# Scores of two heads in the two halves of TensorE's rows, and the first layer's memory products one group of self heads later

## Chip, cores, metric

One core of one Trainium2 chip. The metric is the device time of one execution in microseconds (us). In every stretch quoted below the granted TensorE clock is 1.00, its 2.4 GHz level.

## What is computed

A trunk of two layers on 256 tokens of width 1024, in fp32. Each layer mixes tokens with 12 self heads of width 64 and 4 heads that look into 256 memory tokens, adds the output projection to the residual stream, and then runs a SwiGLU layer of width 2816. The first layer's self attention adds a running sum of log gates, the second a distance penalty. Cut to one layer's mixing:

```python
proj = rms_norm(h, norm_mix[i]) @ w_in          # queries, keys, values of 12 heads, memory queries (and gates)
mkv = rms_norm(mem, norm_mem[i]) @ w_mem_kv[i]  # keys and values of 4 memory heads
s = q @ k.T * 64 ** -0.5 + F[t] - F[s]          # first layer; the second: - slope * (t - s); causal
self_out = softmax(s) @ v
mem_out = softmax(qm @ mk.T * 64 ** -0.5) @ mv
h = h + concat(self_out, mem_out) @ w_out[i]
h = h + (silu(hn @ w_gate) * (hn @ w_up)) @ w_down[i]
```

## The kernel before

All products keep fp32 accuracy with fp32r operands: a matrix is split into `hi`, its rounding, and `lo`, the rest, and a product is three matmuls (hi·hi, lo·hi, hi·lo, `prod`). ScalarE (ACT) writes `hi`, VectorE (DVE) the difference `lo`; that is done for activations as well as for the weights, which are streamed from memory in units of up to 1 MB (`Plan`, `fetch`, L207) and split in halves up to five halves ahead of use (`split`, L227 and L230).

TensorE (PE) and SyncE (SP) run in the order in which the code is written (`manual_schedule`, L770); for ACT, DVE and GpSimd (POOL) a scheduler sets the order, save at the start of the first layer. While PE works through the projections, it calls `step()` (L464) after every two k-blocks, which moves each active head pair one step on. `attend` (L394) is such a pair: it lets `idle` steps pass (table `IDLE`, L58), writes the scores of two heads into two PSUM banks (L405 to L409), then DVE and ACT do the softmax (L412 to L431); two or three steps later PE transposes the probabilities (L438), ACT and DVE copy them out of PSUM (L442, L443), and two steps later PE multiplies by the values (L447 to L451). The value products go into halves of the array's columns, 64 for each head (`128*64` in the profile); all other products use the array whole (`128*128`).

A score product contracts over 64 values only. Before the change the other 64 rows are filled so that one matmul does two of the three terms: rows of the head's own half hold `hi` of its queries and the other half holds `lo` (`split_queries`, L378), against keys whose `hi` stands in both halves and whose `lo` stands in one, with zeros beside it (`split_keys`, L386; `no_lo`, L334). A pair so takes eight matmuls of 256 columns, and its operands take six ACT copies and two DVE and two POOL subtractions of 64x256, and two POOL memsets.

In the first layer the order is: values, queries and keys of group 0 of the self heads (two pairs in a group), then `memory_heads` (L547: memory keys and values, L343, and memory queries), then groups 1 and 2 (`MEM_AT`, L55), then the output projection in the order 3, 0, 1, 2 of its row blocks (block 3 is that of the memory heads, L609). The second layer has the same order, with its memory keys and values made earlier, after the first layer's SwiGLU. The gates' running sums go through memory: `gate_sums` (L515) multiplies them out on PE, writes `fr` to `fd` (L522) and reads it back to all partitions as `fk` (L528), which the first layer's softmax needs (`bias`, L530).

Of the kernel before, what the change touches and what calls it, by code (L numbers as in the profile page):

```python
# [22 lines left out]
F32 = mybir.dt.float32  # L23
# [59 lines left out]
class Plan:  # L83


    def __init__(self, a):
# [4 lines left out]
        for i in range(2):  # L91
# [8 lines left out]
            for g in range(3):  # L100
# [5 lines left out]
                U["qk", i, g] = [self.unit([w[:, :SW], w[:, SW:]], 4 * u, 4, g * 2 * P, 2 * P) for u in range(2)]  # L106
            U["out", i] = [self.unit([a["w_out"][i]], 2 * j, 2, 0, D) for j in (3, 0, 1, 2)]
            U["gu", i], U["dn", i] = {}, {}
# [33 lines left out]
def trunk(ctx: ExitStack, tc: tile.TileContext, plan, stream, x, gains, norm_final, square, mem, out):  # L142
# [22 lines left out]

    mem_t = [ap.tile([P, 2, 512], F32, tag="probs", name=f"mem{t}", bufs=3).rearrange("p a s -> p (a s)") for t in range(NT)]

# [77 lines left out]
    def split_ps(hi, lo, ps, scale=None):  # L245

        if scale is None:
            nc.scalar.activation(hi, ps, AF.Copy)
            nc.vector.tensor_sub(lo, ps, hi.bitcast(F32))  # L249
# [79 lines left out]
    fk = cp.tile([P, H, S], F32, name="fk")  # L329
    mks = [cp.tile([P, 2, 2 * S], F32R, name=f"mk{p}") for p in range(HM // 2)]  # L330
# [3 lines left out]
    def no_lo(dst):  # L334

        for a in range(2):
            nc.gpsimd.memset(dst[HOME[1 - a], a, S:].bitcast(F32), 0.0)

# [4 lines left out]
    def mem_kv(i):  # L343
# [31 lines left out]

    ENG = (nc.gpsimd, nc.vector)

    def split_queries(dst, q):  # L378

        for a in range(2):  # L380
            nc.scalar.activation(dst[HOME[a], a], q[HOME[a]], AF.Copy)
        for a in range(2):
            r = ENG[a].tensor_sub(dst[HOME[1 - a], a], q[HOME[a]], dst[HOME[a], a].bitcast(F32))
        return r

    def split_keys(dst, k):  # L386

        for a in range(2):
            nc.scalar.activation(dst[HOME[a], a, :S], k[HOME[a]], AF.Copy)
            nc.scalar.activation(dst[HOME[1 - a], a, :S], k[HOME[a]], AF.Copy)  # L390
        for a in range(2):
            ENG[a].tensor_sub(dst[HOME[a], a, S:], k[HOME[a]], dst[HOME[a], a, :S].bitcast(F32))

    def attend(name, xq, xk, vt, h0, idle, bias, dst, kt):  # L394

# [8 lines left out]
        sb = [bank(f"s_{name}_{a}") for a in range(2)]  # L404
        for a in range(2):  # L405
# [5 lines left out]
        pr = ap.tile([P, 2, 512], F32, tag="probs", name=f"p_{name}", bufs=3)  # L411
        with tc.high_priority(offset=URGENT):  # L412
# [26 lines left out]
        pT = ap.tile([P, 2, 512], F32, tag="probs", name=f"pT_{name}", bufs=3)  # L439
        width = len(blocks) * P  # L440
# [29 lines left out]
    def mixer(i, xs, rs):  # L470
# [44 lines left out]
        def gate_sums():  # L515
            yield
            fb = bank("F_ps")
            fb.mm(fb.t[:H, 0:S], lf[:, 0], prefix)
            fb.mm(fb.t[:H, P:S], lf[:, 1], prefix[:, 0:P], stop=True)
            fr = ap.tile([P, 2, S], F32, tag="work", name="fr", bufs=WORK_BUFS)[:H, 0]  # L520
            nc.vector.tensor_copy(fr, fb.t[:H, :S])
            nc.sync.dma_start(fd, fr)  # L522
            wake_exp(fr[:, 0:1])
            yield
            yield
            for g in range(GATE_PARTS):
                hs = slice(g * (H // GATE_PARTS), (g + 1) * (H // GATE_PARTS))
                nc.sync.dma_start(fk[:, hs], fd[hs].unsqueeze(0).to_broadcast([P, H // GATE_PARTS, S]))  # L528

        def bias(h0):  # L530

            b = fk[:, h0:h0 + 2]
            if i == 1:
                return b[:, :, P:], b

            b0 = ap.tile([P, 2, P], F32, tag="bias", name=f"bias{h0}", bufs=1)
            for t, o in enumerate((b0, b[:, :, P:])):
                with tc.issue_after(mem_done[i]):
                    nc.vector.tensor_add(o, b[:, :, t * P:(t + 1) * P], mask[:, P:].unsqueeze(1).to_broadcast([P, 2, P]))
            return b0, b  # L540
# [6 lines left out]
        def memory_heads():  # L547
# [14 lines left out]
            qm = ap.tile([P, 2, S], F32, tag="work", name=f"qm{i}", bufs=WORK_BUFS)  # L562
            nc.vector.tensor_mul(qm, qb.t.rearrange("p (a s) -> p a s", a=2), rsb[:, 0:1, :].to_broadcast([P, 2, S]))
            for p in range(HM // 2):
                xq = ap.tile([P, 2, S], F32R, tag="work", name=f"xqm{i}{p}", bufs=WORK_BUFS)
                mem_done[i] = split_queries(xq, qm[:, p]).ins
                active.append(attend(f"m{i}{p}", xq, mks[p], mvs, 2 * p, IDLE_MEM[i] + p, None, hT, 6 + p))

        for g in range(3):
# [3 lines left out]
            for k in range(KD):  # L573
# [6 lines left out]
                if k % 2:  # L580
                    step()
            if i == g == 0:
                rs_mem.extend(factor(mem_t[t], f"mem{t}") for t in range(NT))
# [4 lines left out]
            for a in range(2):  # L588
                p = 2 * g + a
                qk = ap.tile([P, 2, S], F32, tag="work", name=f"qk{i}{p}", bufs=WORK_BUFS)  # L590
                nc.vector.tensor_mul(qk.rearrange("p a s -> p (a s)"), kb[a].t, rsb.rearrange("p a s -> p (a s)"))
                xq = ap.tile([P, 2, S], F32R, tag="work", name=f"xq{i}{p}", bufs=WORK_BUFS)
                xk = ap.tile([P, 2, 2 * S], F32R, tag="pair", name=f"xk{i}{p}", bufs=PAIR_BUFS)
                no_lo(xk)
                split_queries(xq, qk[:, 0])
                split_keys(xk, qk[:, 1])
                idle = a + IDLE[i][g]
                active.append(attend(f"s{i}{p}", xq, xk, vsb, 2 * p, idle, bias, hT, p))

# [8 lines left out]

        for n, j in enumerate((3, 0, 1)):  # L609
            for kk in range(2):  # L610
# [34 lines left out]
    def ffn(i, xs, late):  # L645
# [5 lines left out]
        def gu(c, kk):  # L651
# [13 lines left out]
            if first:  # L665
                rsb.append(spread(rs, f"f{i}", (1.0,), "f")[:, 0])
            if kk == 0:
# [102 lines left out]
    with tc.manual_schedule(engines={PE, SP}):  # L770
        warm = ap.tile([P, 512], BF16, tag="work", name="warm", bufs=WORK_BUFS)
        nc.gpsimd.memset(warm, 0.0)
        for mk in mks:
            no_lo(mk)
        wb = bank("warm_ps")
# [47 lines left out]
```

## Time and profile before

| | |
|---|---|
| median of three runs | 621.79 us (621.36 to 622.78) |
| the profiled execution: time, span | 621.42 us, 619.6 us |
| busy share of the span: PE, DVE, ACT, POOL | 98%, 73%, 63%, 10% |
| matmuls | 3634 |

How to read the rows: matmuls are pipelined. One of 256 columns is shown as taking 0.28 us, but in an undisturbed row of them one starts every 0.12 us. A stall of PE therefore shows an idle time that is 0.16 us shorter than the time lost. "Chain" is the chain of waits that ended last: at each step the work that the end was waiting for.

### The profile page before, as it was taken

What the parts mean: (1) busy time and instruction counts of PE and PEld (TensorE: products, weight loads), DVE (VectorE), ACT (ScalarE), POOL (GpSimd) and SP (SyncE); (2) the same over time, 40 slices, a digit from 0 to 9 for tenths busy, and PEclk for the clock granted to TensorE, in tenths of its full rate; (3) what the DMA queues carried; (4) which work ended last, traced back from release to release, by engine and by line L of the source; (5) the groups of instructions that cost most, each with busy time, mean ns of one, the idle gap of its engine ahead of it and who ended that gap; (6) DMA issues with size and microseconds to landing.
All of it is one profiled execution on the core that took longest, in us unless ns stands there. A gap on an engine that the chain in (4) does not pass through costs nothing.

```text
span 619.6 us, 9546 instructions
## 1 busy us (share of the span) xinstructions
PE 606.8 (98%) x3634; PEld 533.0 (86%) x3634; DVE 452.7 (73%) x815; ACT 393.2 (63%) x736; POOL 63.4 (10%) x90
## 2 busy tenths in 40 slices
PE   9999899999999999999999999999999999999995
PEld 6999888788888888888899998877888888888884
DVE  5677999687676776668675589986866766667664
ACT  6889788485555555557467589776755555555542
POOL 2032112055000000000011032110000000000000
PEclk9999999999999999999999999999999999999999
DMA  8977452335544554556355731332445555456301
GB/s 349 422 283 278 165 179 95 135 137 204 199 172 179 197 204 181 177 190 227 126 200 191 272 137 69 136 136 103 170 177 197 205 195 178 177 197 205 136 1 68
DMA packets 16774, 112.31 MB, mean 181 GB/s; under 512 B 1996, under 2 KB 2008, under 8 KB 4312
## 3 DMA queue, kind: packets, MB, share of 16 engines
q1 hardware_dynamic: 16440, 111.42, 49.0%
q8 instruction: 28, 0.46, 0.3%
q10 hardware_dynamic: 288, 0.29, 0.1%
q14 instruction: 18, 0.15, 0.1%
HBM read 110.64 MB, written 1.06 MB: 180 GB/s over the span
## 4 chain that ended last, share of the span: by engine, by line
PE 88%; DVE 5%; ACT 4%; issue 2%; POOL 0%; POOLq 0%; DVEq 0%; ACTq 0%
PE gu L183 40%; PE d_acc L183 18%; PE qk_ps L183 8%; PE o_acc L183 7%; PE v_ps L183 6%; DVE lo L230 2%; PE s_s L183 1%; ACT hi L227 1%; PE pT_s L438 1%; PE o_s L183 1%; PE mv_ps L183 1%; PE qm_ps L183 1%; PE mk_ps L183 1%; PE warm_ps L183 1%; DVE p_m L431 1%
## 5 line engine op out<-in xcount | busy, mean ns | idle before, releaser
L230 DVE TENSOR_TENSOR lo<-raw,hi 128x1024 fp32r<-128x1024 f32 (+3 forms) x201 | 239.7, 1198 | 67.0 <-ACT hi L227 62.1
L227 ACT ACTIVATE hi<-raw 128x1024 fp32r<-128x1024 f32 (+3 forms) x201 | 206.5, 1035 | 71.3 <-PE d_acc L183 46.8
L183 PE MATMUL gu<-x_ffn,hi 128*128 128x512 f32 x704 | 177.4, 392 | 0.0
L183 PEld LDWEIGHTS gu<-x_ffn,hi 128*128 128x128 f32 x704 | 126.3, 189 | 22.2
L183 PE MATMUL d_acc<-hi,h 128*128 128x512 f32 x348 | 107.1, 389 | 0.0
L183 PEld LDWEIGHTS gu<-x_ffn,lo 128*128 128x128 f32 x704 | 96.7, 190 | 8.1 <-ACT x_ffn L251 1.0
L183 PE MATMUL gu<-x_ffn,lo 128*128 128x256 f32 x704 | 100.5, 284 | 0.1
L183 PEld LDWEIGHTS d_acc<-hi,h 128*128 128x128 f32 x348 | 65.3, 188 | 13.6
L183 PE MATMUL qk_ps<-x_x,hi 128*128 128x256 f32 x384 | 72.4, 284 | 2.1 <-ACT p_m L427 2.1
L183 PE MATMUL d_acc<-lo,h 128*128 128x512 f32 x174 | 67.7, 389 | 0.0
L183 PEld LDWEIGHTS qk_ps<-x_x,hi 128*128 128x128 f32 x384 | 61.0, 191 | 3.3 <-ACT p_m L427 2.5
L183 PE MATMUL qk_ps<-x_x,lo 128*128 128x256 f32 x192 | 54.3, 283 | 0.0
L672 ACT ACTIVATE gate<-gu 128x256 f32<-128x256 f32 x44 | 16.9, 384 | 57.6 <-PE gu L183 57.6
L672 ACT ACTIVATE up<-gu 128x256 f32<-128x256 f32 x44 | 16.9, 385 | 39.7 <-PE gu L183 39.5
L183 PE MATMUL o_acc<-hi,x_hT 128*128 128x512 f32 x128 | 41.6, 404 | 0.3 <-DVE x_hT L249 0.3
L183 PEld LDWEIGHTS d_acc<-lo,h 128*128 128x128 f32 x174 | 32.7, 188 | 6.8
L673 DVE TENSOR_TENSOR gate<-gu,gate 128x256 f32<-128x256 f32 x44 | 18.7, 424 | 25.6 <-ACT gate L672 25.5
L183 PEld LDWEIGHTS qk_ps<-x_x,lo 128*128 128x128 f32 x192 | 36.8, 191 | 0.0
L673 DVE TENSOR_TENSOR up<-gu,up 128x256 f32<-128x256 f32 x44 | 18.7, 424 | 24.6 <-ACT up L672 24.6
L183 PE MATMUL v_ps<-hi,x_x 128*128 128x384 f32 (+1 forms) x128 | 33.1, 339 | 0.0
L183 PEld LDWEIGHTS o_acc<-hi,x_hT 128*128 128x128 f32 x128 | 22.9, 188 | 5.9 <-DVE x_hT L249 1.0
L427 ACT ACTIVATE p_s<-p_s,nmax_s 128x128 f32<-128x128 f32 (+1 forms) x48 | 21.3, 445 | 9.8 <-DVE nmax_s L417 9.7
(152 smaller groups left out, 752.2 us busy)
## 6 DMA issues: line engine op xcount, KB each, us to landing
raw<-in_stream SPq DMA_DIRECT2D x94, 1024.0 KB, 4.8
raw<-in_stream SPq DMA_DIRECT2D x3, 1036.0 KB, 7.9
raw<-in_stream SPq DMA_DIRECT2D x4, 768.0 KB, 4.5
fk<-fd SPq DMA_DIRECT2D x3, 512.0 KB, 7.5
raw<-in_stream SPq DMA_DIRECT2D x2, 518.0 KB, 4.4
h<-in_x SPq DMA_DIRECT2D x2, 512.0 KB, 11.9
mem<-in_mem SPq DMA_DIRECT2D x2, 512.0 KB, 12.5
gfin<-in_norm_final SPq DMA_DIRECT2D x1, 512.0 KB, 3.6
```

What stands on the lines that cost most here:

```text
L183: nc.tensor.matmul(o, lhsT, rhs, start=self.fresh, stop=stop, skip_group_check=True)
L227: nc.scalar.activation(hi[:, c0:c1], src[:, c0:c1], AF.Copy)
L230: nc.vector.tensor_sub(lo[:, c0:c1], src[:, c0:c1], hi[:, c0:c1].bitcast(F32))
L427: nc.scalar.activation(pr[:, a, c], src, AF.Exp, bias=nmax[:, a, j], scale=scale, accum_out=total[:, a, j])
L431: nc.vector.tensor_scalar_mul(pr[:, a, c], pr[:, a, c], rc[:, a, qt:qt + 1])
L438: nc.tensor.transpose(tb[a].t[:, n * P:(n + 1) * P], pr[:, a, c:c + P], ident)
L672: nc.scalar.activation(v[:, 1], b[s].t[:, S:], AF.Copy)
L673: nc.vector.tensor_add(v[:, 0], b[s].t[:, :S], v[:, 1])
```

## The change

1. `split_queries`, `split_keys`, `no_lo` and the duplicated operands go. `split_ps` (one ACT copy and one DVE subtraction, L245) splits a pair's queries and keys together in one 128x512 operation each, so head 0 lies in partitions 0 to 63 and head 1 in 64 to 127; the four memory heads' keys are split the same way (`mks`), and their queries too (`xm`). POOL has no part in it any more.
2. `attend` makes twelve score matmuls for a pair instead of eight, each on 64 rows by 128 columns of the array, those of the two heads in turn.
3. The first layer's memory products move behind group 1 (`MEM_AT`); its `IDLE` tables and the order of its output projection are set to suit (`OUT_ORDER`), and `gate_sums` starts one step earlier. In the second layer the tables' values stay what they were.
4. `probs` gets four buffers (was three). A pair's operands (`xp`, `xm`) take one `pair` buffer of three.

```diff
-MEM_AT = (1, 1)
+MEM_AT = (2, 1)
-IDLE = ((7, 2, 2), (3, 2, 2))
-IDLE_MEM = (1, 1)
+IDLE = (((5, 6), (4, 5), (2, 3)),
+        ((3, 4), (2, 3), (2, 3)))
+IDLE_MEM = ((2, 3), (1, 2))
+OUT_ORDER = ((0, 1, 3, 2), (3, 0, 1, 2))
...
-        for p in range(HM // 2):
-            split_keys(mks[p], mk[:, p])
+        split_ps(mks[:, 0], mks[:, 1], mk)
...
-        for a in range(2):
-            for qt in range(NT):
-                o, q = sb[a].t[:, qt * S:(qt + 1) * S], slice(qt * P, (qt + 1) * P)
-                sb[a].mm(o, xq[:, a, q], xk[:, a, :S])
-                sb[a].mm(o, xq[:, a, q], xk[:, a, S:], stop=True)
+        for qt in range(NT):
+            o, q = slice(qt * S, (qt + 1) * S), slice(qt * P, (qt + 1) * P)
+            for n, (st, mv) in enumerate(((xq[0], xk[0]), (xq[1], xk[0]), (xq[0], xk[1]))):
+                for a in range(2):
+                    sb[a].mm(sb[a].t[:, o], st[HOME[a], q], mv[HOME[a]], stop=n == 2)
...
         def gate_sums():
-            yield
             fb = bank("F_ps")
...
-                xq = ap.tile([P, 2, S], F32R, tag="work", name=f"xq{i}{p}", bufs=WORK_BUFS)
-                xk = ap.tile([P, 2, 2 * S], F32R, tag="pair", name=f"xk{i}{p}", bufs=PAIR_BUFS)
-                no_lo(xk)
-                split_queries(xq, qk[:, 0])
-                split_keys(xk, qk[:, 1])
+                xp = ap.tile([P, 2, 2, S], F32R, tag="pair", name=f"xp{i}{p}", bufs=PAIR_BUFS)
+                split_ps(xp[:, 0], xp[:, 1], qk)
```

PE in the first layer, where the first self pair's scores (`s_s`) stand. Before, after the fourth k-block of group 1, beside a memory pair's (`s_m`):

```order
L183 MATMUL qk_ps_753<-x_x_81,hi_0_629 128x256
L183 MATMUL s_s_0_871<-xk_485,xq_484 128x256 x4
L183 MATMUL s_s_1_872<-xk_485,xq_484 128x256 x4
L183 MATMUL s_m_0_899<-mk_87,xqm_747 128x256 x4
L183 MATMUL s_m_1_900<-mk_87,xqm_747 128x256 x4
```

In the changed program, the last two of the twelve, which now stand between memory keys and values (`mk_ps`, `mv_ps`):

```order
L185 MATMUL s_s_0_704<-xp_465 128x256
L185 MATMUL s_s_1_705<-xp_465 128x256
L185 MATMUL mk_ps_633<-x_mem_626,hi_0_513 128x256
L185 MATMUL mk_ps_633<-x_mem_626,lo_0_514 128x256
L185 MATMUL mk_ps_633<-x_mem_626,hi_0_513 128x256 x2
```

The first scores moved from group 1's projection to the middle of the memory keys, and the two heads alternate. Over the whole first layer the scores now stand alone between products on the whole array five times, and beside a value product three times; in the second layer four times alone (once two pairs together), three times beside one value product or between two.

ACT in the first layer, at the split of group 0's first pair. Before:

```order
L227 ACTIVATE hi_0_376<-raw_328 128x1024
L227 ACTIVATE hi_2_404<-raw_328 128x1024
L381 ACTIVATE xq_484<-qk_482 64x256
L389 ACTIVATE xk_485<-qk_482 64x256
L390 ACTIVATE xk_485<-qk_482 64x256
```

and in the changed program:

```order
L229 ACTIVATE hi_0_429<-raw_331 128x1024
L250 ACTIVATE xp_465<-qk_463 128x512
L250 ACTIVATE xp_470<-qk_468 128x512
L229 ACTIVATE hi_2_475<-raw_331 128x1024
L253 ACTIVATE x_mem_626<-raw_321,gT 128x256
```

One row for a pair stands where six copies were.

DVE in the second layer, from the memory queries (`qm`) to the maxima of the first memory pair's scores (`nmax_m`). Before:

```order
L563 TENSOR_TENSOR qm_3823<-qm_ps_3764,rsb_x_3729 128x512
L392 TENSOR_TENSOR xk_3751<-qk_3748,xk_3751 64x256
L230 TENSOR_TENSOR lo_2_3838<-raw_3565,hi_2_3837 128x1024
L383 TENSOR_TENSOR xqm_3825<-qm_3823,xqm_3825 64x256
L383 TENSOR_TENSOR xqm_3830<-qm_3823,xqm_3830 64x256
L230 TENSOR_TENSOR lo_0_3868<-raw_3638,hi_0_3867 128x1024
L230 TENSOR_TENSOR lo_2_3924<-raw_3638,hi_2_3923 128x1024
L420 TENSOR_REDUCE nmax_m_3905<-s_m_0_3895 128x1 x2
L420 TENSOR_REDUCE nmax_m_3905<-s_m_1_3896 128x1 x2
```

and in the changed program:

```order
L541 TENSOR_TENSOR qm_3735<-qm_ps_3676,rsb_x_3663 128x512
L232 TENSOR_TENSOR lo_0_3773<-raw_3572,hi_0_3772 128x1024
L251 TENSOR_TENSOR xm_3737<-qm_3735,xm_3737 128x512
L232 TENSOR_TENSOR lo_2_3833<-raw_3572,hi_2_3832 128x1024
L232 TENSOR_TENSOR lo_0_3927<-raw_3630,hi_0_3926 128x1024
L399 TENSOR_REDUCE nmax_m_3814<-s_m_0_3800 128x1 x2
L399 TENSOR_REDUCE nmax_m_3814<-s_m_1_3801 128x1 x2
```

Three subtractions of 64x256 went and one of 128x512 came; three weight splits stand on the way in both.

SP's queue in the first layer, from the memory loads (`mem`) to the gates' way through memory (`fd`, `fk`). Before (raw_237 and raw_328 are the memory heads' key and value weights, raw_340 to raw_555 those of groups 1 and 2):

```order
L207 DMA raw_237<-in_stream 128x2048
L199 DMA mem_79<-in_mem 128x1024
L199 DMA mem_80<-in_mem 128x1024
L207 DMA raw_328<-in_stream 128x2048
L207 DMA raw_338<-in_stream 128x2048
L207 DMA raw_340<-in_stream 128x2048
L207 DMA raw_374<-in_stream 128x2048
L207 DMA raw_432<-in_stream 128x2048
L207 DMA raw_555<-in_stream 128x2048
L522 DMA fd<-fr 12x256
L207 DMA raw_627<-in_stream 128x2048
L528 DMA fk<-fd 128x1024 x3
```

and in the changed program, where group 1's two units stand ahead of this piece, raw_321 is the memory itself, raw_331 and raw_367 its weights, raw_427 and raw_511 group 2:

```order
L209 DMA raw_321<-in_stream 128x2048
L209 DMA raw_331<-in_stream 128x2048
L201 DMA mem_79<-in_mem 128x1024
L201 DMA mem_80<-in_mem 128x1024
L209 DMA raw_367<-in_stream 128x2048
L209 DMA raw_425<-in_stream 128x2048
L209 DMA raw_427<-in_stream 128x2048
L500 DMA fd<-fr 12x256
L209 DMA raw_511<-in_stream 128x2048
L506 DMA fk<-fd 128x1024 x3
```

The memory's transfers moved behind group 1's, and the gates' write went one unit forward, ahead of group 2's second unit.

## Rows read from the trace of the kernel before

**Rows 1.** Page, part 1: busy us (share of the span) and instructions

```profile
PE 606.8 (98%) x3634; PEld 533.0 (86%) x3634; DVE 452.7 (73%) x815; ACT 393.2 (63%) x736; POOL 63.4 (10%) x90
```

**Rows 2.** Stretches: busy us of PE, PEld, DVE, ACT, POOL; clock; DMA share, GB/s

```profile
48.00:60.00 12.00, 12.00 (x102) 12.00 (x102) 8.54 (x10) 11.60 (x21) 1.95 (x3) 1.00 0.79 290
60.00:66.00 6.00, 5.15 (x43) 4.95 (x42) 5.94 (x10) 3.18 (x5) 1.99 (x2) 1.00 1.01 393
72.00:78.00 6.00, 4.09 (x33) 3.88 (x33) 5.92 (x27) 5.78 (x21) 1.90 (x2) 1.00 0.00 0
78.00:96.00 18.00, 18.00 (x142) 15.46 (x141) 17.88 (x48) 14.89 (x36) 4.22 (x6) 1.00 0.50 177
376.00:382.00 6.00, 4.87 (x42) 4.66 (x41) 5.89 (x19) 5.64 (x16) 1.89 (x2) 1.00 0.48 176
```

**Rows 3.** Timeline of PE at its stalls: start, us, [idle before, what ended it]

```profile
60.03 0.28 PE L183 MATMUL qk_ps<-x_x,hi 128*128 128x256 f32 x1
61.16 1.10 PE L183 MATMUL s_m<-mk,xqm 128*128 128x256 f32 x7 [0.85 <-POOL xqm L383]
...
73.04 0.38 PE L183 MATMUL qk_ps<-x_x,hi 128*128 128x256 f32 x1 [1.18 <-ACT p_m L427]
...
74.89 0.39 PE L183 MATMUL qk_ps<-x_x,hi 128*128 128x256 f32 x1 [0.88 <-ACT p_m L427]
...
379.18 0.63 PE L438 MATMUL pT_m<-sq,p_m 128*128 128x128 f32 x4 [1.14 <-DVE nmax_s L417]
```

**Rows 4.** Chain of waits in order of time: start us, us, what

```profile
23.95 11.51 PE qk_ps L183 x96
...
78.19 2.87 PE qk_ps L183 x24
...
81.71 1.02 PE o_m L183 x8
82.73 3.07 PE qk_ps L183 x24
...
101.27 0.95 PE s_s L183 x8
```

**Rows 5.** Timeline of PE and PEld in narrow windows at one value product

```profile
86.39 0.43 PE L183 MATMUL o_m<-pT_m,mv 128*64 128x256 f32 x1
...
86.39 0.44 PE L183 MATMUL o_m<-pT_m,mv 128*64 128x256 f32 x2
...
86.39 0.66 PE L183 MATMUL o_m<-pT_m,mv 128*64 128x256 f32 x4
...
86.39 0.13 PEld L183 LDWEIGHTS o_m<-pT_m,mv 128*64 128x64 f32 x1 [0.17 <-DVE lo L230]
...
86.39 0.15 PEld L183 LDWEIGHTS o_m<-pT_m,mv 128*64 128x64 f32 x2 [0.17 <-DVE lo L230]
```

**Rows 6.** Groups by line and shape: xcount | busy us, mean ns | idle before

```profile
L227 ACT ACTIVATE hi<-raw 128x1024 fp32r<-128x1024 f32 x184 | 193.0, 1056 | 62.2 <-PE d_acc L183 46.8 <-PE qk_ps L183 6.3 <-PE o_acc L183 6.1
...
L389 ACT ACTIVATE xk<-qk 64x256 fp32r<-64x256 f32 x24 | 10.0, 416 | 0.4
L381 ACT ACTIVATE xq<-qk 64x256 fp32r<-64x256 f32 x24 | 10.0, 415 | 4.1 <-DVE qk L591 3.7
...
L383 DVE TENSOR_TENSOR xq<-qk,xq 64x256 fp32r<-64x256 f32 x12 | 8.1, 678 | 1.5 <-ACT xq L381 1.2
L591 DVE TENSOR_TENSOR qk<-qk_ps,rsb_x 128x512 f32<-128x512 f32 x12 | 8.0, 679 | 1.6 <-ACT rsb_x L283 1.6
...
L392 DVE TENSOR_TENSOR xk<-qk,xk 64x256 fp32r<-64x256 f32 x12 | 5.8, 481 | 1.2 <-ACT xk L389 0.9
```

**Rows 7.** Timeline of SP's queue, and the page's DMA issues (last: us to landing)

```profile
48.20 0.43 SPq L522 DMA_DIRECT2D fd<-fr  x1
...
52.92 1.28 SPq L528 DMA_DIRECT2D fk<-fd  x3
...
fk<-fd SPq DMA_DIRECT2D x3, 512.0 KB, 7.5
```

More of the change, by code (lines that the diff above doesn't have):

```diff
@@ L106, in __init__ @@
                 U["qk", i, g] = [self.unit([w[:, :SW], w[:, SW:]], 4 * u, 4, g * 2 * P, 2 * P) for u in range(2)]
-            U["out", i] = [self.unit([a["w_out"][i]], 2 * j, 2, 0, D) for j in (3, 0, 1, 2)]
+            U["out", i] = [self.unit([a["w_out"][i]], 2 * j, 2, 0, D) for j in OUT_ORDER[i]]
             U["gu", i], U["dn", i] = {}, {}
@@ L163, in trunk @@
     nc.gpsimd.memset(minus_half, -0.5)
-    mem_t = [ap.tile([P, 2, 512], F32, tag="probs", name=f"mem{t}", bufs=3).rearrange("p a s -> p (a s)") for t in range(NT)]
+    mem_t = [ap.tile([P, 2, 512], F32, tag="probs", name=f"mem{t}", bufs=4).rearrange("p a s -> p (a s)") for t in range(NT)]
     def load_x():
@@ L329, in trunk @@
     fk = cp.tile([P, H, S], F32, name="fk")
-    mks = [cp.tile([P, 2, 2 * S], F32R, name=f"mk{p}") for p in range(HM // 2)]
+    mks = cp.tile([P, 2, HM // 2, S], F32R, name="mks")
     mvs = [cp.tile([P, HM, DH], F32, name=f"mv{t}") for t in range(NT)]
     HOME = [slice(a * DH, (a + 1) * DH) for a in range(2)]
-    def no_lo(dst):
-        for a in range(2):
-            nc.gpsimd.memset(dst[HOME[1 - a], a, S:].bitcast(F32), 0.0)
     rs_mem = []
@@ L373, in mem_kv @@
         yield
[L376 to L392, printed above, removed]
     def attend(name, xq, xk, vt, h0, idle, bias, dst, kt):
@@ L404, in attend @@
         sb = [bank(f"s_{name}_{a}") for a in range(2)]
-        for a in range(2):
-            for qt in range(NT):
-                o, q = sb[a].t[:, qt * S:(qt + 1) * S], slice(qt * P, (qt + 1) * P)
-                sb[a].mm(o, xq[:, a, q], xk[:, a, :S])
-                sb[a].mm(o, xq[:, a, q], xk[:, a, S:], stop=True)
+        for qt in range(NT):
[3 more added lines that the diff above has]
+                    sb[a].mm(sb[a].t[:, o], st[HOME[a], q], mv[HOME[a]], stop=n == 2)
         nmax = sp.tile([P, 2, NT], F32, tag="nmax", name=f"nmax_{name}")
-        pr = ap.tile([P, 2, 512], F32, tag="probs", name=f"p_{name}", bufs=3)
+        pr = ap.tile([P, 2, 512], F32, tag="probs", name=f"p_{name}", bufs=4)
         with tc.high_priority(offset=URGENT):
@@ L537, in bias @@
             for t, o in enumerate((b0, b[:, :, P:])):
-                with tc.issue_after(mem_done[i]):
+                with tc.issue_after(mem_done[i]) if i in mem_done else nullcontext():
                     nc.vector.tensor_add(o, b[:, :, t * P:(t + 1) * P], mask[:, P:].unsqueeze(1).to_broadcast([P, 2, P]))
@@ L563, in memory_heads @@
             nc.vector.tensor_mul(qm, qb.t.rearrange("p (a s) -> p a s", a=2), rsb[:, 0:1, :].to_broadcast([P, 2, S]))
+            xm = ap.tile([P, 2, HM // 2, S], F32R, tag="pair", name=f"xm{i}", bufs=PAIR_BUFS)
+            mem_done[i] = split_ps(xm[:, 0], xm[:, 1], qm).ins
             for p in range(HM // 2):
-                xq = ap.tile([P, 2, S], F32R, tag="work", name=f"xqm{i}{p}", bufs=WORK_BUFS)
-                mem_done[i] = split_queries(xq, qm[:, p]).ins
-                active.append(attend(f"m{i}{p}", xq, mks[p], mvs, 2 * p, IDLE_MEM[i] + p, None, hT, 6 + p))
+                active.append(attend(f"m{i}{p}", (xm[:, 0, p], xm[:, 1, p]), (mks[:, 0, p], mks[:, 1, p]), mvs, 2 * p,
+                                     IDLE_MEM[i][p], None, hT, 6 + p))
         for g in range(3):
@@ L581, in mixer @@
                     step()
-            if i == g == 0:
+            if i == 0 and g == MEM_AT[0] - 1:
                 rs_mem.extend(factor(mem_t[t], f"mem{t}") for t in range(NT))
@@ L591, in mixer @@
                 nc.vector.tensor_mul(qk.rearrange("p a s -> p (a s)"), kb[a].t, rsb.rearrange("p a s -> p (a s)"))
-                xq = ap.tile([P, 2, S], F32R, tag="work", name=f"xq{i}{p}", bufs=WORK_BUFS)
-                xk = ap.tile([P, 2, 2 * S], F32R, tag="pair", name=f"xk{i}{p}", bufs=PAIR_BUFS)
-                no_lo(xk)
-                split_queries(xq, qk[:, 0])
-                split_keys(xk, qk[:, 1])
-                idle = a + IDLE[i][g]
-                active.append(attend(f"s{i}{p}", xq, xk, vsb, 2 * p, idle, bias, hT, p))
+                xp = ap.tile([P, 2, 2, S], F32R, tag="pair", name=f"xp{i}{p}", bufs=PAIR_BUFS)
+                split_ps(xp[:, 0], xp[:, 1], qk)
+                idle = IDLE[i][g][a]
+                active.append(attend(f"s{i}{p}", (xp[:, 0, 0], xp[:, 1, 0]), (xp[:, 0, 1], xp[:, 1, 1]), vsb, 2 * p, idle, bias, hT, p))
         acc = [[bank(f"o_acc{i}{t}{c}") for c in range(2)] for t in range(NT)]
@@ L607, in o_item @@
                 prod(acc[t][c], acc[t][c].t, tok(hT, k, t), (wh[:, 0, cs], wl[:, 0, cs]), n == 3 and kk == 1)
-        for n, j in enumerate((3, 0, 1)):
+        for n, j in enumerate(OUT_ORDER[i][:3]):
             for kk in range(2):
@@ L772, in trunk @@
         nc.gpsimd.memset(warm, 0.0)
-        for mk in mks:
-            no_lo(mk)
         wb = bank("warm_ps")
```

6 lines of the change are left out of this document (3 added, 3 removed).

## Prediction

> **What bounds the kernel now.** I read the page's busy shares first, then busy times by stretch, then the timeline of PE alone where a stretch shows it idle, and the chain of waits for prices. PE is busy 98% of the span [rows 1], at the full clock, and undisturbed it starts a matmul of 256 columns every 11.51 / 96 = 0.12 us [rows 4]. So two things alone can move the end: what PE itself has to do, and the few places where it stands still. In both layers these lie in the attention. In the first layer PE loses time between 60 and 78 us, in the second between 376 and 382 us [rows 2]. In each of these stretches DVE is busy nearly without a break (5.94, 5.92 and 5.89 of 6.00 us), while from 48 to 60 us, just before, it has 3.5 us of 12 free [rows 2]. DVE's work is not too much for the layer, it is bunched.
>
> The stalls, one by one [rows 3]. A matmul of 256 columns is shown with 0.28 us and starts every 0.12, so a stall costs its idle time and 0.16 us, and about 0.1 more, since the first matmul behind it shows 0.38 where others show 0.28. First layer: the memory scores wait for POOL's part of the query split, 0.85 idle; group 2's projection waits twice for the exponentials of the second memory pair, whose two score banks it is to reuse, 1.18 and 0.88 idle. That is 0.85 + 1.18 + 0.88 + 3 x 0.26 = **3.7 us**. Second layer: the second memory pair's transposes wait for DVE, 1.14 + 0.26 = **1.4 us**. Together 5.1 us.
>
> **The change part by part.**
>
> *Splits.* For one self pair ACT now makes six copies of 0.416 us, 2.5 us [rows 6]. Then it makes one of 128x512; between the copy of 256 columns (0.416) and the one of 1024 (1.056) [rows 6] that is about 0.63, so 1.9 us less. DVE makes 0.68 + 0.48 = 1.16 us now and then one subtraction of 128x512, about 0.68 by the product of that shape [rows 6]: 0.5 us less. With six self pairs a layer that is 11 us of ACT and 3 us of DVE, and the memory pairs give some on top. None of it is on PE's path for itself; it counts only at the stalls. POOL's part goes to nothing, and with it the 0.85 us wait.
>
> *The second layer's stall.* Nothing is moved there, the tables keep their values. On the way from the memory queries to the first maxima DVE loses two subtractions for one, and in PE's order the next places are the same. DVE is full from there to the stall, so what it saves ahead of the maxima (two subtractions, one of them waiting for POOL) moves the transposed probabilities forward by at least the 1.14 us that they are late. I take the whole 1.4 us.
>
> *The first layer's stalls.* Group 1's projection now comes straight after group 0's, the first self scores stand in the middle of the memory keys, about 23.95 + 2 x 11.51 + 48 x 0.12 = 53 us [rows 4] instead of behind the memory scores at 61 [rows 3], so two softmaxes fall into the stretch where DVE had 3.5 us free, and group 2's projection no longer takes the banks of the second memory pair. All three causes go. What is late next: the memory pairs now come last before the output projection, and the second one's probabilities are wanted by PE one value product, one transposition and twelve output matmuls later, some 5 us. That is close for a softmax, so I keep half of the longest stall back, 0.7 us. Taken: 3.7 - 0.7 = 3.0 us. The memory's transfers move behind group 1's units on SP, which are wanted first then; the transfers are as many as before.
>
> *Scores on PE.* No row shows a matmul on 64 of the 128 rows; the nearest are the value products on 64 of the columns. There [rows 5] one matmul alone takes 0.43 us, two take 0.44, four 0.66: two heads run side by side, 0.01 apart, and the next two follow 0.22 later. Their weight loads overlap too (0.13 for one, 0.15 for two). If the rows' halves do the same, twelve matmuls are six pairs of 0.12 = 0.72 us, where eight took 0.95 [rows 4]: 0.23 less for each of 16 pairs of heads (twelve self, four memory), **3.7 us less**. If they don't, a pair is 0.24 and the score product 1.44, 0.49 more.
>
> Going over to halves is not free. A value product of four such pairs takes 1.02 us in the chain where 4 x 0.22 = 0.88 is its own, 0.14 for going in; the projection after it takes 3.07 instead of 2.87 [rows 4], 0.20 for coming out. So an excursion costs 0.34. In the changed order the first layer's scores make five excursions of their own and three times add one change to a value product's: 5 x 0.34 + 3 x 0.20 = 2.3 us. In the second layer four of their own (two pairs share one) and two single changes; at the eighth place they stand between two value products, where there are two changes already: 4 x 0.34 + 2 x 0.20 = 1.8. Together **4.1 us more**. For row halves this price could be nothing (0) or, if each change costs as much as coming out, 9 x 0.40 + 5 x 0.20 = 4.6; I take 4.1, the column halves' own.
>
> The Trainium skill speaks to the first of these (TensorE: Matmul & The Clock Gate, Part 3, Measured speedup): four row tiles together ran 3.07 times as fast as alone, not four times. By that ratio, as an estimate, a pair would cost 0.12 x 4 / 3.07 = 0.156 us and the whole gain on scores would be gone. Rows 5 show full overlap for column halves; no row here shows row halves. The next part has its mechanism among the rivals.
>
> *Sum.* -3.0 - 1.4 - 3.7 + 4.1 = -4.0 us. The profiled execution took 621.42 us, 0.37 below the median of the three runs, so about 617.4 there and **617.8 us** against the median.
>
> **The rivals.**
>
> *The halves run one after another* (the side on which it is slower). At each of 16 score products six pairs then cost 0.24 and not 0.12: 16 x 6 x 0.12 = 11.5 us, 629.3. It decides from 0.12 + 4.0 / 96 = 0.16 us a pair on: above that the change loses. For it: each head's matmul has a weight load of 128 columns of its own, twice as long as the value products' 64, and there is only 0.12 us to hide two of them. Against: rows 5.
>
> *Half side by side*: a pair of 0.16, a third of the way from 0.12 to 0.24, costs 96 x 0.04 = 3.8 us, 621.6, no change. For it: the same loads, partly hidden. Against: in rows 5 the second head's load adds 0.02 us, not a third.
>
> *The first layer's stalls come back elsewhere.* The first softmax now needs `fk` some 10 us earlier. Before, `fd` was issued at 48.2, `fk` 4.7 us later, and it landed 7.5 us after that [rows 7], at 60.4. The scores at 53 us are wanted transposed three steps on, 3 x 2.87 [rows 4] and a score product, at 63; if the softmax takes half of that way (an estimate), `fk` has to be there by 58 and `fd` issued by 46. PE makes the sums 24 matmuls, 2.9 us, earlier than before, but SP still holds `fd` back behind a weight unit that waits for a buffer. And in DVE's order whatever waits for `fk` holds the weight splits behind it. If this or the memory pairs at the end cost 3 us again, 620.8 remains, no change.
>
> *Row halves change over for nothing*: 4.1 us less, 613.7. For it: rows show a price only where columns are halved, and there the accumulation side changes as well. Against: nothing that a row shows.
>
> *The change does not do what it says* can be ruled out in one respect only: the order shows the two heads alternating. Whether they overlap is the first rival.
>
> **How the numbers follow.** Forecast (616 to 619.5) 0.53; changing over for nothing 0.10; stalls elsewhere 0.13; half side by side 0.12; one after another 0.12. The range goes from the free change at 613.6 to 621.8, which takes in the forecast, the returned stalls and part of the half-overlap, and leaves the serial case out. A measurement of this kernel can tell about 0.2%, 1.24 us, from no change. Faster than 620.55: 0.53 + 0.10, and 0.07 from the lower parts of the two middle cases, 0.70. Slower than 623.03: 0.12 and a little of the half-overlap, 0.14. Between: 0.16.
>
> **What would show it.** In the changed profile a score product between whole-array products should span about 0.72 us plus 0.14, and the matmul group after it 0.20 more than without; single starts should come in twos, 0.01 apart, 0.12 between twos. If they come evenly at 0.12 the first rival holds. PE should be without idle between 40 and 78 us and at the second layer's transposes of the memory probabilities; an idle PE before the first transposes, ended by DVE, would be `fk`; before the second memory pair's transposes in the first layer, the softmax at the end. POOL should have nothing in the attention, and DVE some free time where it was full. The SwiGLU stretches should be the same to 0.1 us; a difference there would mean that I looked in the wrong place.

## The result, and the profile after

The changed kernel takes 617.70 us (median of 617.51 to 617.83), the kernel before in the same comparison 622.28 us: a ratio of 0.9931, 95% interval 0.9918 to 0.9943, so 4.6 us less. The profiled execution's span is 615.6 us where it was 619.6: from one execution to the next the kernel before comes out near 621.4 or near 622.9 us, and its profile is of the lower of the two, so the profiles account for 4.0 of the 4.6 us. Forecast were 617.8 us and a range of 613.6 to 621.8; the total was met, but two of its terms were put down to the wrong part of the change.

The first part of the page of the changed kernel, in the form of [rows 1]:

```profile
PE 606.5 (99%) x3698; PEld 530.1 (86%) x3698; DVE 441.7 (72%) x799; ACT 363.6 (59%) x656; POOL 24.3 (4%) x30
```

DVE has lost 11 us of work, ACT 30, POOL 39. PE's own work is as it was (606.8 to 606.5), with 64 matmuls more. The waits of PE in the whole span, by what it waited for (us in total, times, longest):

```profile
PE warm_ps L185 <- POOL warm L748: 1.3, 1, 1.3
PE o_acc L185 <- DVE x_hT L251: 0.3, 2, 0.2
```

Both are in the kernel before too; every wait of [rows 3] is gone. The same stretches as in [rows 2] (the last one moved by the 3 us that the second layer starts earlier): busy us of PE, PEld, DVE, ACT, POOL, then clock, DMA share and GB/s.

```profile
48.00:60.00 12.00, 12.00 (x108) 11.46 (x107) 11.23 (x23) 6.86 (x12) 0.00 (x0) 1.00 1.01 376
60.00:66.00 6.00, 6.00 (x52) 5.88 (x51) 6.00 (x25) 5.17 (x17) 0.00 (x0) 1.00 0.76 306
72.00:78.00 6.00, 6.00 (x55) 5.45 (x55) 6.00 (x21) 3.46 (x11) 0.00 (x0) 1.00 0.20 51
78.00:96.00 18.00, 18.00 (x147) 15.19 (x144) 14.99 (x39) 11.87 (x30) 0.00 (x0) 1.00 0.28 104
373.00:379.00 6.00, 6.00 (x54) 6.00 (x53) 5.83 (x22) 5.61 (x18) 0.00 (x0) 1.00 0.08 30
```

PE is busy in all of them. DVE works now in 48 to 60, where it had 3.5 us free, and has 3 us free in 78 to 96, where it was full. The scores, in two narrow windows of PE's timeline and then the whole product (start, us, what):

```profile
54.12 0.38 PE L185 MATMUL s_s<-xp 64*128 64x256 f32 x1
...
54.12 0.39 PE L185 MATMUL s_s<-xp 64*128 64x256 f32 x2
...
54.12 0.50 PE L185 MATMUL s_s<-xp 64*128 64x256 f32 x4
...
54.12 0.98 PE L185 MATMUL s_s<-xp 64*128 64x256 f32 x12
```

One matmul takes 0.38 us, two take 0.39, four 0.50: the two row halves work side by side, and the next two follow 0.12 later. The chain of waits at a score product (start, us, what), beside [rows 4]:

```profile
66.12 0.91 PE s_s L185 x12
67.03 3.06 PE qm_ps L185 x24
70.09 2.88 PE qk_ps L185 x24
```

A score product takes 0.91 us where eight whole matmuls took 0.95, and the projection behind it 3.06 where one that nothing disturbs takes 2.88. So on PE the row halves bring almost nothing. The gain is elsewhere, and for the rest of the study I read it by stage: the **attention** of a layer runs from its first `qk_ps` matmul to its first `gu` matmul. For the changed kernel the timeline of PE shows these two starts in the first layer and in the second:

```profile
23.87 0.28 PE L185 MATMUL qk_ps<-x_x,hi 128*128 128x256 f32 x1
...
123.11 0.36 PE L185 MATMUL gu<-x_ffn,lo 128*128 128x256 f32 x1
...
337.50 0.28 PE L185 MATMUL qk_ps<-x_x,hi 128*128 128x256 f32 x1
...
423.78 0.36 PE L185 MATMUL gu<-x_ffn,lo 128*128 128x256 f32 x1
```

That is 99.24 and 86.28 us. All other stages are the same to 0.2 us, but for the start: the first layer's attention begins between 23.55 and 24.28 us, one way or the other from execution to execution. The table holds every kernel of this study, read in the same way; the times of different comparisons lie up to 1.1 us apart (the kernel before came out between 621.6 and 622.7), the stages of kernels that share a layer's code agree to 0.1. A tenth of a microsecond is thus told by a stage, not by a time.

| kernel | first layer's attention | second layer's | time, us | ratio to before, 95% |
|---|---|---|---|---|
| before | 102.51 | 87.21 | 622.28 | |
| changed | 99.24 | 86.28 | 617.70 | 0.9918 to 0.9943 |
| operands only | 98.78 | 86.25 | 616.58 | 0.9897 to 0.9924 |
| move undone | 98.76 | 86.27 | 616.63 | 0.9898 to 0.9926 |
| move only | 103.75 | 85.91 | 621.24 | 0.9979 to 0.9997 |
| fourth buffer only | 102.46 | 85.89 | 620.42 | 0.9968 to 0.9989 |
| halves not in turn | 101.98 | 88.27 | 622.16 | 0.9994 to 1.0013 |
| whole-array scores | 96.76 | 84.00 | 612.57 | 0.9831 to 0.9858 |
| operands, ACT's work back | 100.26 | 86.41 | 619.03 | 0.9936 to 0.9964 |
| operands, DVE's work back | 98.79 | 86.27 | 617.07 | 0.9905 to 0.9933 |
| operands, POOL's work back | 98.74 | 86.69 | 617.43 | 0.9911 to 0.9938 |
| paired, order of the change | 99.79 | 85.01 | 616.57 | 0.9897 to 0.9928 |
| paired, order of before | 98.20 | 85.00 | 615.04 | 0.9872 to 0.9910 |
| the last, group 2 earlier | 98.68 | 85.90 | 616.42 | 0.9890 to 0.9917 |

### The profile page after: what moved, and what is told of

Its sections match the earlier page's. It is cut to its first block, busy times and chain, and to the rows that moved or that the text cites. A ratio compares the mean times of both kernels' runs of the same rounds, so it can differ in the third digit from the quotient of the medians.

```text
span 615.6 us, 9472 instructions
## 1 busy us (share of the span) xinstructions
PE 606.5 (99%) x3698; PEld 530.1 (86%) x3698; DVE 441.7 (72%) x799; ACT 363.6 (59%) x656; POOL 24.3 (4%) x30
## 4 chain that ended last, share of the span: by engine, by line
PE 95%; DVE 2%; ACT 1%; DMA 1%; issue 0%; POOLq 0%; ACTq 0%
PE gu L185 40%; PE d_acc L185 19%; PE qk_ps L185 11%; PE o_acc L185 7%; PE v_ps L185 6%; PE mk_ps L185 2%; PE qm_ps L185 2%; PE mv_ps L185 2%; PE s_s L185 1%; PE pT_s L417 1%; PE o_s L185 1%; DVE lo L232 1%; PE o_m L185 1%; DMA raw<-in_stream 1%; ACT hi L229 1%; PE pT_m L417 0%
```

## The experiments

### The two halves of the change apart

Operands only, as an edit of the changed kernel:

```diff
-MEM_AT = (2, 1)
+MEM_AT = (1, 1)
-IDLE = (((5, 6), (4, 5), (2, 3)),
+IDLE = (((7, 8), (2, 3), (2, 3)),
-IDLE_MEM = ((2, 3), (1, 2))
-OUT_ORDER = ((0, 1, 3, 2), (3, 0, 1, 2))
+IDLE_MEM = ((1, 2), (1, 2))
+OUT_ORDER = ((3, 0, 1, 2), (3, 0, 1, 2))
         def gate_sums():
+            yield
```

(and three `probs` buffers in place of four). Move only is the kernel before with these lines the other way round and four `probs` buffers.

> Half of the change: the new operands and the row-half scores (split_ps for queries and keys, no POOL work), in the order of before (memory products in front of group 1, the old tables, three probability buffers, the gate sums one step later). Theory A, the first layer's stalls are due to the engines' work: the 0.85 us wait for POOL goes (0.85 + 0.26 = 1.1 us) and DVE, with 1.16 us less to 0.68 a pair ahead of the softmaxes, also shortens the two waits for the memory exponentials, together about 2.6 us in the first layer and 0.8 in the second, with row halves neutral on PE: about 618.9. Theory B, they are due to the order: only the 1.1 us and the second layer's 0.8 go, the two waits for p_m stay at 1.2 and 0.9 us: about 620.4.

> The other half: the order of the change (memory products between groups 1 and 2, the new tables, four probability buffers, no leading step in the gate sums), with the operands and the eight whole-row score matmuls a pair of before. Theory B (order): the three stalls of the first layer go (3.2 us), the second layer keeps its 1.4 us at the transposes: about 619.1. Theory A (work of DVE, ACT and POOL): POOL and DVE are as full as before, PE stands idle again in the first layer, by half or more of the 3.7 us, most likely at the memory pairs that now come last: 620.5 or more.

Measured: 616.58 us and 621.24 us. Theory B has fallen in both, and theory A's figure for the operands, 618.9, was 2.3 us too high. The operands alone take 3.73 us off the first layer's attention, more than the whole change does (3.27), and PE has no wait left there; the move alone makes that stage 1.24 us longer than before. Its waits:

```profile
PE s_m L185 <- DVE x_hT L251: 1.5, 1, 1.5
PE warm_ps L185 <- POOL warm L773: 1.3, 1, 1.3
PE o_s L185 <- ACT p_m L429: 1.0, 1, 1.0
PE o_acc L185 <- DVE x_hT L251: 0.3, 2, 0.2
PE pT_s L440 <- DVE p_s L433: 0.3, 1, 0.3
```

So the order does get rid of the three stalls of [rows 3], and with the old operands it made three others, 1.5, 1.0 and 0.3 us, two of them at the memory pairs, which now come last: where the prediction had kept 0.7 us back. And they cost more than their idle time. The windows of the move-only kernel there, in the columns of [rows 2]:

```profile
84.00:90.00 6.00, 4.49 (x38) 4.23 (x36) 6.00 (x15) 2.52 (x5) 0.00 (x0) 1.00 0.58 193
90.00:92.00 2.00, 1.02 (x8) 0.55 (x8) 1.91 (x6) 1.94 (x9) 0.00 (x0) 0.83 0.86 365
92.00:96.00 4.00, 4.00 (x21) 3.14 (x18) 3.87 (x10) 3.89 (x12) 1.47 (x2) 0.66 0.14 57
96.00:102.00 6.00, 6.00 (x37) 4.40 (x35) 5.67 (x14) 5.92 (x16) 1.31 (x2) 1.00 0.00 0
```

After the idle 1.51 and 0.97 us the granted clock is 0.83 and 0.66 for six microseconds, that is, a part of them at the 1.2 GHz level. By these figures the lower clock cost up to 2 x 0.17 + 4 x 0.34 = 1.7 us (an estimate), so a good part of what the move lost with the old operands. The stalls of [rows 3], up to 1.18 us, left the clock at 1.00 in [rows 2], and so did a single wait of 1.68 us in a run below.

Then the move undone alone, with the fourth buffer kept:

> The changed kernel with the move alone undone: memory products in front of group 1 and the tables, output order and gate sums of before, but four probability buffers and all else as changed. If the move costs what the counted changes between whole and half arrays say (29 in the first layer with it, 26 without, 3 x 0.19 = 0.57 us) and hides no stall, the first layer's attention takes 98.7 us where the changed kernel takes 99.2, and the time is about 617.1 or, by the operands-only run, 616.6. If the move is worth something that the operands-only run hid: over 617.7.

Measured: 616.63 us, 98.76 us for the first layer's attention, 0.48 less than in the changed kernel. The move hides nothing once the operands are changed; it costs 0.5 us. Counted in PE's order there are 29 changes between whole and half arrays with it and 26 without, and 3 x 0.19 us is 0.57.

### What the row halves cost

Two heads not in turn, six matmuls of head 0 and then six of head 1:

```diff
-        for qt in range(NT):
-            o, q = slice(qt * S, (qt + 1) * S), slice(qt * P, (qt + 1) * P)
-            for n, (st, mv) in enumerate(((xq[0], xk[0]), (xq[1], xk[0]), (xq[0], xk[1]))):
-                for a in range(2):
+        for a in range(2):
+            for qt in range(NT):
+                o, q = slice(qt * S, (qt + 1) * S), slice(qt * P, (qt + 1) * P)
+                for n, (st, mv) in enumerate(((xq[0], xk[0]), (xq[1], xk[0]), (xq[0], xk[1]))):
                     sb[a].mm(sb[a].t[:, o], st[HOME[a], q], mv[HOME[a]], stop=n == 2)
```

> The changed kernel, with the two heads of a pair not in turn: six matmuls of head 0, then six of head 1. If the two row halves work side by side only where a matmul of the other half stands next in the queue, 16 score products lose the overlap of five of their six twos, 16 x 5 x 0.12 = 9.6 us more than the changed kernel, 627.3, and single starts come 0.12 apart. If each half has a queue of its own that runs ahead, nothing changes: 617.7.

Measured: 622.16 us, 4.5 more than the changed kernel, half of the 9.6. The chain has a score product at 1.25 us where it was 0.91, 0.34 more. In the first layer that is all of it, 8 x 0.34 = 2.7 of 2.74 us. The second is only 1.99 us longer: two products stand together there and lose it once, and the short wait of the changed kernel (below, with the fourth buffer) is gone.

```profile
74.54 1.25 PE s_s L185 x12
```

Four windows that open at the first of its matmuls, on PE's timeline, show why:

```profile
54.02 0.62 PE L185 MATMUL s_s<-xp 64*128 64x256 f32 x3
...
54.02 0.73 PE L185 MATMUL s_s<-xp 64*128 64x256 f32 x4
...
54.02 0.74 PE L185 MATMUL s_s<-xp 64*128 64x256 f32 x5
...
54.02 0.85 PE L185 MATMUL s_s<-xp 64*128 64x256 f32 x6
```

They end 0.11 or 0.12 us apart, but the fourth and fifth 0.01. Two matmuls that run together must be on different halves, and all six of head 0 stand first in the code; so one of head 1 runs here beside head 0's third or fourth, ahead of its turn. (The records do not name the half, so this is worked out, not read.) In all, the product takes 9 slots of 0.12 us and not 12 or 6: PE runs ahead, but only by about three matmuls. The alternation in the code is worth 4.5 us, and neither of the two answers that I had set out was right.

Whole-array scores, the same number of array slots without halves:

```diff
-            for n, (st, mv) in enumerate(((xq[0], xk[0]), (xq[1], xk[0]), (xq[0], xk[1]))):
-                for a in range(2):
-                    sb[a].mm(sb[a].t[:, o], st[HOME[a], q], mv[HOME[a]], stop=n == 2)
+            for a in range(2):
+                sb[a].mm(sb[a].t[:, o], xq[0][:, q], xk[0])
+            sb[qt].mm(sb[qt].t[:, o], xq[1][:, q], xk[1], stop=True)
```

> The changed kernel with each score product's twelve row-half matmuls replaced by six matmuls on all 128 rows and 256 columns, which add the two heads' scores together (so what is computed changes: no head has scores of its own), in the same places and with the same reads and banks. Same time on the array, 6 x 0.12 = 0.72 us, without going over to halves. If the change over costs 0.19 each way (9 lone excursions x 0.38 and 5 single changes x 0.20 = 4.4 us): about 613.3. If row halves change over for nothing, and what the changed kernel's rows show there has another cause: 617.7.

Measured: 612.57 us, 5.1 less. Its chain, at the place of the rows of the changed kernel above:

```profile
65.11 0.71 PE s_s L185 x6
65.83 2.88 PE qm_ps L185 x24
68.70 2.88 PE qk_ps L185 x24
```

0.71 for 0.91, and 2.88 for 3.06: going over to row halves costs 0.20 and coming back 0.18. With the scores on the whole array there are 16 changes left in the first layer in place of 29 and 14 in place of 24 in the second; 23 x 0.19 = 4.4 us, and 0.34 us more go in the second layer, where the changed kernel has a new short wait (below, with the fourth buffer). Together 4.7 of the 4.8 us that the two stages show. Changing over for nothing, one of the rivals, is out.

### What took the stalls away

The operands-only kernel with work that one engine saved given back, as dead work (cut to the lines for a self pair; less is given back for the memory queries):

```diff
+nc.scalar.activation(junk[0][HOME[j % 2]], qk[HOME[j % 2], j // 2], AF.Copy)   # four
...
+nc.vector.tensor_sub(junk[0][HOME[0]], qk[HOME[0], 0], qk[HOME[0], 1])
...
+nc.gpsimd.memset(junk[j][HOME[j]], 0.0)                                        # two
+nc.gpsimd.tensor_sub(junk[j][HOME[1 - j]], qk[HOME[1 - j], 0], qk[HOME[1 - j], 1])   # two
```

> The operands-only kernel (616.6 us, no idle PE in the first layer's attention) with ACT's saved work given back as dead work: four copies of 64x256 into a spare tile behind each self pair's split (4 x 0.416 = 1.7 us) and two behind the memory queries' split; nothing reads them. If it was ACT's relief that took the first layer's stalls away, PE stands idle again for the memory exponentials, 2 us or more: 618.6 or later. If it was DVE's, or the wait for POOL and the order of the splits, ACT has room (24 of 72 us free between 40 and 112): 616.6 to 617.2.

> The operands-only kernel with DVE's saved work given back as dead work: one subtraction of 64x256 (0.48 to 0.68 us) for each self pair and one for the memory queries, into a spare tile that nothing reads. If DVE's queue set the first layer's stalls, it is pushed back by 0.5 us a pair where it is full (60 to 78 us) and some idle PE returns, 0.5 to 2 us: 617.1 to 618.6. If it did not: 616.6.

> The operands-only kernel with POOL's work given back as dead work: two memsets and two subtractions of 64x256 for each self pair, two subtractions for the memory queries, into spare tiles that nothing reads and nobody waits for. If POOL at work beside DVE slows DVE enough to matter, DVE's means rise by some per cent and the time goes to 617 or more. If POOL counted only where it was waited for: 616.6.

Measured: 619.03, 617.07 and 617.43 us. DVE's subtraction by itself changes nothing: the attention stages are those of the operands-only kernel to 0.02 us, and its 0.5 us in the time stand ahead of them (the first layer's attention starts at 24.28, there at 23.61). POOL's work costs nothing in the first layer and 0.4 in the second. ACT's work does cost, 1.48 us in the first layer, in one wait on PE's timeline:

```profile
77.35 0.82 PE L418 MATMUL pT_s<-sq,p_s 128*128 128x128 f32 x6
79.45 1.09 PE L185 MATMUL o_m<-pT_m,mv 128*64 128x256 f32 x8 [1.28 <-ACT pT_m L422]
```

The value product waits for ACT's copy of the transposed probabilities, not for the exponentials as in [rows 3]. Of the 3.7 us the wait for POOL's part, which no longer exists, is 1.1 by [rows 3], and the ACT work given back here is worth 1.5, though at another wait. The rest, about 1.1 us, no experiment here took apart, and the three runs together are not the whole relief. They give work back one engine at a time: the dead subtraction takes DVE 0.41 us, where the two for the memory queries took 0.90 each in the kernel before, beside POOL. And none of them gives back the split of the memory keys. In the kernel before, the chain that ends with the second wait for the exponentials runs through it (start, us, what):

```profile
52.97 0.42 ACT mk L389
...
56.03 0.43 ACT mk L390
56.47 1.07 ACT hi L227
...
60.55 0.72 DVE xqm L383
...
73.86 0.99 ACT p_m L427 x4
```

ACT copies the memory keys in eight pieces, from 52.97 to 56.46 us; a weight split, the memory queries and DVE's subtractions for them follow, and DVE's maxima of the memory scores start at 65.58. In the operands-only kernel the keys take one copy of 0.64 us, and the maxima start at 62.46. So the operands as a whole took the stalls away; what part of that was ACT's, DVE's or POOL's stays open.

The second layer, where nothing moves, by the fourth buffer alone (and one small tile moved to make room for it):

```diff
-        pr = ap.tile([P, 2, 512], F32, tag="probs", name=f"p_{name}", bufs=3)
+        pr = ap.tile([P, 2, 512], F32, tag="probs", name=f"p_{name}", bufs=4)
```

> The kernel before with one thing of the change alone: four buffers for probabilities in place of three (and the broadcast reciprocal of the feed-forward part in the tile of the attention's, for room). In the move-only run the second layer's attention took 85.9 us where the kernel before takes 87.2, with tables and operands as before there. If the fourth buffer does that, the 1.4 us at the second layer's transposes goes here too, and the first layer's stalls may shrink with it: 620.4 or less. If it does not: 621.8.

Measured: 620.42 us; the second layer's attention is 85.89 for 87.21, 1.3 of the stall's 1.4, and the first layer's is unchanged, with its three waits. On DVE the last scaling of the second memory pair's probabilities, in the kernel before and in this one:

```profile
376.86 1.62 DVE L431 TENSOR_SCALAR p_m<-p_m,rc_m 128x256 f32<-128x256 f32 x2
```

```profile
375.98 0.60 DVE L431 TENSOR_SCALAR p_m<-p_m,rc_m 128x256 f32<-128x256 f32 x2
```

With a free buffer the scheduler places this scaling, and the first of a self pair's maxima, ahead of a weight split of 1.20 us, and all but the end of the scaling then comes before POOL's subtraction, beside which it fell in the kernel before. The operands-only kernel, with three buffers, has lost the same stall (86.25). So the second layer's gain has two sufficient causes, and the prediction named one.

It is not whole in the changed kernel. Behind the second memory pair's transposes group 2's projection starts late:

```profile
370.58 1.09 PE L417 MATMUL pT_m<-sq,p_m 128*128 128x128 f32 x8
371.81 0.39 PE L185 MATMUL qk_ps<-x_x,hi 128*128 128x256 f32 x1
```

Eight transposes that start 0.11 us apart leave PE free at about 371.47, so 0.34 us are lost that show no idle time, because a matmul shows 0.16 more than its slot. Where ACT is slower, in the run with its work back, the same place is listed as a wait, for the exponentials of [rows 3]:

```profile
PE qk_ps L185 <- ACT p_m L407: 0.3, 1, 0.3
```

### Fewer changes

If each change costs 0.19 us, two pairs at the same step should save four of the eight that two pairs make. In the changed kernel's order, and in the order of before with four buffers:

```diff
-IDLE = (((5, 6), (4, 5), (2, 3)), ((3, 4), (2, 3), (2, 3)))
-IDLE_MEM = ((2, 3), (1, 2))
+IDLE = (((5, 5), (4, 4), (2, 2)), ((3, 3), (2, 2), (2, 2)))
+IDLE_MEM = ((2, 2), (1, 1))
...
+IDLE = (((7, 7), (2, 2), (2, 2)), ((3, 3), (2, 2), (2, 2)))   # with MEM_AT = (1, 1)
+IDLE_MEM = ((1, 1), (1, 1))
```

> The changed kernel with the two pairs of a group at the same step (equal idles in the tables), so that their score products stand next to each other, and their transposes and value products too: 17 changes between whole-array and half-array matmuls in place of 29 in the first layer, 16 in place of 24 in the second. Theory: each change costs 0.19 to 0.20 us of PE and nothing else moves, 20 x 0.19 = 3.8 us less than the changed kernel, 613.9. Rival: two softmaxes at once bunch DVE and ACT, PE stands idle before the second pair's transposes, 1 us or more at several of the eight places: 616 to 620.

> The same pairing on the operands-only kernel (memory products in front of group 1) with four probability buffers: 18 changes in place of 26 in the first layer, 16 in place of 24 in the second. Theory: 16 x 0.19 = 3.0 us less than the operands-only kernel, 613.6. Rival as above, at its worst for the memory pairs and group 1, whose four score products then stand within 5 us: 616 to 620.

Measured: 616.57 and 615.04 us, where the theory had 613.9 and 613.6. The second is the fastest in the table but for the whole-array scores: by stages 1.04 and 1.28 us less than the changed kernel. In its chain two pairs make one score product, and one projection pays for it:

```profile
83.83 1.62 PE s_s L185 x24
85.45 3.06 PE qk_ps L185 x24
88.51 1.50 PE o_s L185 x16
```

1.62 us for two products that took 0.91 each. The rival took part of the gain in both. At the end of either layer the output product waits longer for the last value product's split, in the changed kernel and here:

```profile
116.45 0.50 PE L185 MATMUL o_acc<-hi,x_hT 128*128 128x512 f32 x1 [0.17 <-DVE x_hT L251]
```

```profile
115.42 0.50 PE L185 MATMUL o_acc<-hi,x_hT 128*128 128x512 f32 x1 [0.58 <-DVE x_hT L251]
```

That is 0.4 us a layer. In the order of the change the memory pairs, close together and last, also wait for their probabilities, so its first layer is longer than unpaired (99.79 for 99.24):

```profile
91.96 0.50 PE L417 MATMUL pT_m<-sq,p_m 128*128 128x128 f32 x2 [1.68 <-DVE p_m L410]
```

I tried to win the 0.4 us back:

> The kernel with paired heads in the old order (615.0 us), group 2's scores one step earlier in both layers (idle 1 for 2), so that the last value product stands one output step further from the output matmuls that read it. There PE lost 0.86 us in each layer, 0.42 more than with separate pairs. Theory: both waits go back to 0.44 us or less, 2 x 0.42 = 0.8 us gained, 614.2. Rival: the scores now stand 5 us behind the end of the projection that feeds them and DVE's split is not ready, or the softmaxes of groups 1 and 2 collide on DVE: 615.0 or later.

Measured: 616.42 us, 1.4 more. My premise was wrong: with one idle step less the last value products still fall behind the last output step, so the wait stayed (0.86 us a layer). The attentions are 0.48 and 0.90 us longer, with PE losing time just before and within group 2's scores, as the rival's first half has it.

## Why the prediction was right, and where it was not

- **What bounds the kernel** held. The SwiGLU stretches are the same to 0.1 us, and the whole gain is in the two attentions, 3.27 and 0.93 us.
- **Splits.** The ACT copy of 128x512 takes 0.63 us and the DVE subtraction 0.68, as worked out. That this alone would take away the first layer's stalls was not in the sum: I gave it the wait for POOL and left the two waits for the exponentials to the order. That is the step that failed. The operands-only run has all 3.7 us, with the old order; which engine's relief did how much of it is open.
- **The first layer's order.** It was to bring the larger part of 3.0 us. It costs 0.5 on top of the new operands, and with the old ones it makes as many stalls as it removes, and a stretch at the lower clock. The causes named do go; what comes in their place with the old operands, the memory pairs at the end, I had priced at 0.7 us, and with the new ones it is nothing.
- **The second layer's stall** of 1.4 us went, by either the operands or the fourth buffer, which the prediction held for room and nothing more; 0.34 us came back ahead of group 2's projection.
- **Scores.** 0.71 us for 0.72 forecast (without the changes over), 0.24 less a pair, 3.8 in all for 3.7. Halves one after another and half side by side did not happen: a two costs 0.12. The weight loads that spoke for them take 0.18 to 0.19 us in the changed kernel, not twice the 0.13 of [rows 5], and the two of a two overlap.
- **Changing over.** The number of changes was right, 9 x 2 + 5 = 23. Each costs 0.19; in the sum they were 0.14 in and 0.20 out, 4.1 us in all, measured 4.4. So the row halves lose 0.6 us on PE, and pay only through the splits that they allow.
- **`fk`.** `fd` goes out at 43.08, five microseconds earlier than in [rows 7]; `fk` is issued at 47.75 and lands 6.2 us later, and DVE does not wait for it. That rival did not come.
- **Why the sum still fitted.** By its terms the first layer should have lost 3.0 + 8 x 0.23 - 2.3 = 2.5 us and the second 1.4 + 1.8 - 1.8 = 1.4; they lost 3.27 and 0.93. The two errors, 0.7 and 0.5, have opposite signs, and the forecast started from 621.8 us where the kernel before now had 622.3. That the total was met to 0.1 us is luck, and says little about its terms.

## What to carry to other kernels

A change that does two things is worth running in halves even where its sum comes out as forecast: here one half brought all of the gain and the other cost a tenth of it. Before a stall is put down to the order of work, ask whether the engine it waits for would be in time in the old order with its new load. Products on part of the array should stand next to each other: each change to or from them was worth as much as one and a half matmuls, and putting pairs together gave more than the move did.

## What the runs showed of the hardware

- A change between the whole array and row halves costs 0.18 to 0.20 us in either direction; for column halves [rows 4] and [rows 5] give 0.14 in and 0.20 out. The Trainium skill (TensorEngine Tiling (Array Packing), Tiling Modes, Key Properties) says that switching mode drains the engine. The traces show no drain as such, but a cost at every change, as it would make, and its price.
- Two 64-row matmuls of 256 columns, each with its own weights of 128 columns, run at twice the rate of one: 0.39 us for two and 0.38 for one. Where a second score product follows the first, its twelve take 0.70 us, six slots (chain of the operands-only kernel):

```profile
64.09 0.91 PE s_s L185 x12
65.00 0.70 PE s_m L185 x12
```

  The estimate of 0.156 us for two, which the prediction worked out from the ratio of 3.07 in the Trainium skill (TensorE: Matmul & The Clock Gate, Part 3, Measured speedup), is not borne out: it is 0.12.
- Matmuls of one half seem to start ahead of earlier ones that wait for the other half. With the heads not in turn the product takes 1.25 us; in strict order only the sixth and seventh could run together, 0.19 + 11 x 0.12 = 1.51. The Trainium skill (TensorE: Matmul & The Clock Gate, Part 3, The mechanism) has matmuls start strictly in program order; the measured time decides here, and it is shorter. The value products of the kernel before point the same way. There the code writes one head's two matmuls, of 256 and of 128 columns for a self pair, ahead of the other head's, and each leaves two records; but the first four records all have 256 columns, so both heads run from the start (duration in ns, first and last start in us, form):

```profile
L183 PE MATMUL o_s<-pT_s,v x4: 379/404/430, 91.4 to 91.7; 128*64 128x256 f32 x4
```

- POOL at work slows DVE, though nobody waits for POOL. The subtraction of 128x512 takes 0.68 us on average with POOL idle and 0.83 with its work given back, single ones 0.66 to 0.74 or 1.00 to 1.23 (operands only, then with POOL's work; xcount, busy us, mean ns, idle before):

```profile
L251 DVE TENSOR_TENSOR xp<-qk,xp 128x512 fp32r<-128x512 f32 x12 | 8.2, 680 | 0.2
```

```profile
L251 DVE TENSOR_TENSOR xp<-qk,xp 128x512 fp32r<-128x512 f32 x12 | 9.9, 829 | 0.2
```
